# Weight-quarter sums on GpSimd instead of VectorE, and more value blocks through the Strassen path

## The chip, the core and the metric

The kernel runs on one core of one Trainium2 chip. The metric is device microseconds of one execution; the time of the kernel before is the median of three runs. Engines are named as the profile names them: PE (TensorE), DVE (VectorE), ACT (ScalarE), POOL (GpSimd) and SP (SyncE, which here only issues DMAs).

## The reference

Two transformer blocks over 512 tokens of width 1024, all in fp32. The first block is a hybrid attention mixer followed by a convolutional feed-forward stage:

```python
def conv_ffn(h, w_up, conv_w, conv_b, w_down):
    u = h @ w_up
    u = lax.conv_general_dilated(u, conv_w[:, None, :], window_strides=(1,), ...
    gate, val = jnp.split(u, 2, axis=-1)
    return (jax.nn.gelu(gate, approximate=True) * val) @ w_down
```

`w_up` is 1024 x 8192, so there are 4096 gate columns and 4096 value columns. The second block puts 16 meta tokens ahead (528 tokens) and runs two layers, each with two gated feed-forward stages of hidden width 2816 around a mixer:

```python
def swiglu(x, w_gate, w_up, w_down):
    return (jax.nn.silu(x @ w_gate) * (x @ w_up)) @ w_down
```

## The kernel before

**Number format.** Every weight and activation is split into a rounded high part H (a cast on ACT, L177) and a low part L = raw - H (a subtraction on DVE, L178). A product is three matmuls: H by H, H by low, low by H.

**Blocks.** The up-projections are done in blocks of 256 output columns, weights of 128 x 2048 that arrive as two raw tiles (`wraw`, 128 x 1024 each, three buffers). A block is done in one of two ways. The *direct* way (`direct`, gemm at L211) is 2 x 8 x 3 = 48 matmuls of 512 token columns (in the conv stage). The *Strassen* way (`strassen`) takes the 2 x 2 blocking of weights and tokens and needs seven products instead of eight: 7 x 4 x 3 = 84 matmuls of half the token columns (256 in the conv stage, 264 or 256 in the second block; L319 when a product opens an accumulator, L321 when it adds to one). The token side's sums are made once per stage (`strassen_y`). The weight side's four sums are made for each block, each of them one 128 x 512 addition or subtraction:

```python
S[:, :512] = A21 + A22             # L301
S[:, 512:] = S[:, :512] - A11      # L302
A12 = A12 - S[:, 512:]             # L305, in place
A11 = A11 - A21                    # L306, in place
```

S is the tile `ws` (one buffer). The split pieces go to tiles `wq` (four buffers; `w3` is a separate small pool for one quarter in the second block's stages). The order of products on PE is 0, 1, 4, 5, then product 3 of the *previous* block (its tail), then 2 and 6. Products 0 and 1 need the split of the raw r1 = (A11, A12); products 4 and 5 need the split of S; products 2 and 6 need the split of the r1 that L305 and L306 overwrote. On ACT, L330, L335 and L337 copy the accumulators of products 0, 4 and 5 out of PSUM; product 6 adds to the accumulator that L337 reads. On DVE, L333, L342 and L344 add accumulators to these copies.

**Which blocks.** In the conv stage, block b (0 to 15) has a gate part g and a value part v. Before, the gate parts of b = 2 to 14 and the value parts of odd b from 3 to 15 go the Strassen way: 13 + 7 = 20. In each of the four gated stages of the second block, gate and up parts of blocks 2 to 10 do: 4 x 9 x 2 = 72. Together 92.

**What sets the order.** A scheduler orders the instructions of each engine from the program's dependences, tile buffers and its own estimates; each engine then works its list strictly in that order. Between groups of blocks come slices of the down-projection (`down`, L211 on `hid`; accumulated by DVE at L1198 in the conv stage and L1325 in the second block). `conv` (L1134 on ACT, L1137 on DVE) and `hidden` (L1265, L1266) follow each block of the conv stage.

Of the kernel before, what the change touches and what calls it, by code (L numbers as in the profile page):

```python
# [132 lines left out]
class Builder:  # L133
# [157 lines left out]
    def strassen(self, src, Y, R, out, last, off=0, mid=None):  # L291


        nc, h = self.nc, R.n // 2
        r1 = self.wraw(src[:, :1024])
        r2 = self.wraw(src[:, 1024:], *self.rawpool)
        A11, A12, A21, A22 = r1[:, :512], r1[:, 512:], r2[:, :512], r2[:, 512:]
        W = [None] * 7
        W[0], W[1] = self.wtiles(r1, step=1024)
        S = (self.sumpool or self.qp).tile([P, 1024], F32, name="ws", tag="ws", bufs=1)  # L300
        nc.vector.tensor_add(out=S[:, :512], in0=A21, in1=A22)  # L301
        nc.vector.tensor_sub(out=S[:, 512:], in0=S[:, :512], in1=A11)  # L302
        W[4], W[5] = self.wtiles(S, step=1024)
        W[3], = self.wtiles(A22, **(dict(pool=self.qp, tag="w3", bufs=2, cols=512) if self.w3 else {}))
        nc.vector.tensor_sub(out=A12, in0=A12, in1=S[:, 512:])  # L305
        nc.vector.tensor_sub(out=A11, in0=A11, in1=A21)  # L306
        W[6], W[2] = self.wtiles(r1, back=True)

        def product(i, ps=None, tag="g"):

            new = ps is None
            ps = self.psum(tag)[:, :h] if new else ps
            for k in range(4):
                H, L = [t[:, k * P:(k + 1) * P] for t in W[i]]
                yH, yL = Y[i][k]
                for j, (a, b) in enumerate(((H, yH), (H, yL), (L, yH))):
                    first, last = k == 0 and j == 0, k == 3 and j == 2
                    if new:
                        nc.tensor.matmul(ps, lhsT=a, rhs=b, start=first, stop=last)  # L319
                    else:  # L320
                        nc.tensor.matmul(ps, lhsT=a, rhs=b, start=False, stop=last, skip_group_check=True)  # L321
            return ps

        u = self.qp.tile([P, 2, TT // 2], F32, name="cu", tag="cu", bufs=2)
        v = self.qp.tile([P, TT // 2], F32, name="cv", tag="cv", bufs=2)
        u1, u2, v = u[:, 0, :h], u[:, 1, :h], v[:, :h]
        a0, b0 = R.off + off, R.off + off + h
        A, B = slice(a0, b0), slice(b0, b0 + h)
        X = product(0)
        nc.scalar.copy(out=u1, in_=X)  # L330
        out = out()
        Z = product(1, tag="o")
        nc.vector.tensor_add(out=out[:, 0, A], in0=u1, in1=Z)  # L333
        Y5 = product(4)
        nc.scalar.copy(out=v, in_=Y5)  # L335
        product(5, X)
        nc.scalar.copy(out=u2, in_=X)  # L337
        self.end()
        if mid:
            mid()  # L340
        product(2, Y5)
        nc.vector.tensor_add(out=out[:, 0, B], in0=u2, in1=Y5)  # L342
        product(6, X)
        nc.vector.tensor_add(out=out[:, 1, B], in0=v, in1=X)  # L344

        def tail():
            product(3, X)
            last(out[:, 1, A], X)

        self.tail = tail  # L350
        return A, out
# [772 lines left out]
    def conv_ffn(self):  # L1124
        nc, A, R, qp = self.nc, self.A, R1, self.qp
        ys, rb = self.prenorm_end()
        hid, self.hb, self.w3, self.gub = {}, 4, False, 3
        off = 2 - NMETA

        def conv(u, j):  # L1130

            a = qp.tile([P, 2, SEQ], F32, name="ca", tag="ca", bufs=2)
            for n in range(2):
                nc.scalar.activation(out=a[:, n], in_=u[:, n, 2:SEQ + 2], func=AF.Identity, scale=self.v("conv_w2", j + n),  # L1134
                                     bias=self.v("conv_b", j + n))
                for i in (1, 0):
                    nc.vector.scalar_tensor_tensor(out=a[:, n], in0=u[:, n, i:i + SEQ], scalar=self.v(f"conv_w{i}", j + n),  # L1137
                                                   in1=a[:, n], op0=ALU.mult, op1=ALU.add)
            return a

        def direct(u, w, n, Rp):
            for t, o, m in self.gemm(w, n, ys, Rp):
                nc.scalar.copy(out=u[:, n, o + off:o + off + m], in_=t[:, :m])

        def product(b, fast, mid=None):
            if fast:
                a, u = self.strassen(A["w_up"][b], self.Y, R, buf, lambda o, p: nc.scalar.copy(out=o, in_=p), off, mid)
            else:
                if mid:
                    mid()  # L1150
                u = buf()
                w = self.qblock(A["w_up"][b])
                for n in range(2):
                    direct(u, w, n, R)
                    self.end()
            return u

        def post(b, g, v):
            a = conv(g, 2 * b)
            nc.scalar.activation(out=a, in_=a, func=AF.Gelu_apprx_tanh)  # L1160
            c = conv(v, 32 + 2 * b)
            nc.vector.tensor_mul(out=c, in0=c, in1=a)
            hid[2 * b], hid[2 * b + 1] = self.hidden(c, NMETA)

        def buf():
            u = self.gu()
            nc.vector.memset(u[:, :, 0:2], 0.0)
            return u

        def up(b):  # L1170
            if b == 0:
                g, v, hid["g"] = buf(), buf(), buf()
                W = [*self.pre, self.qblock(A["w_up"][1], pool=qp, tag="h", bufs=self.hb, cols=2 * TT, step=1024)]
                self.prenorm_y(self.rlast)
                for Rp in R.parts:
                    for u, w in zip((g, v, hid["g"]), W):
                        for n in range(2):
                            direct(u, w, n, Rp)
            elif b == 1:
                g = hid.pop("g")  # L1180
                v = product(17, False, self.flush)
            else:
                if b == 2:
                    self.Y = self.strassen_y(ys, R, True)
                g = product(b, b < 15)
                v = product(16 + b, b % 2, self.flush)
            self.pending = lambda: post(b, g, v)

        def down(ci, k0, nk, nb):
            W = self.wblock(A[f"w_down{ci}"][nb], nk, step=1024)  # L1190
            for n in range(2):
                t = 2 * nb + n
                ps = self.gemm(W, n, [hid[k0 + k] for k in range(nk)], R, tag="sg"[n])[0][0]
                self.end()
                if k0 == 0:
                    nc.scalar.copy(out=self.x[:, t, NMETA:], in_=ps)
                else:
                    nc.vector.tensor_add(out=self.x[:, t, NMETA:], in0=self.x[:, t, NMETA:], in1=ps)  # L1198

        def last(ci, k0, nk):  # L1200
            W = self.last_w(A[f"w_down{ci}"], nk, ("t3", "t4"))
            hs = [hid[k0 + k] for k in range(nk)]
            self.prenorm("ffn1_norm_0", False)
            acc = self.tmp("acc2", 1)

            def products(R, between=()):
                self.gemm_pairs(W, hs, R, lambda ps, t: self.post_tile(ps, acc, t, R, True), between)

            def post(R):
                self.postnorm(acc, "ffn_post_norm", R, R2.parts[R1.parts.index(R)], self.xd, None)  # L1210

            self.halves(R1.parts, products, post, self.ffn_w("ffn1_0"), R2.parts)

        self.ffn_order(CHUNKS1, up, down, last)

    def last_w(self, src, nk=4, spare=("t3",)):
# [660 lines left out]
```

## Time and profile before

| what | value |
|---|---|
| median of 3 runs | 3096.11 us (3094.0 to 3098.47) |
| profiled execution | 3098.56 us |
| its span, first to last instruction | 3096.8 us |
| mean granted PE clock | 0.996 of full speed |
| PE busy | 3060.1 us, 99% |
| DVE busy | 2191.9 us, 71% |
| ACT busy | 1511.0 us, 49% |
| POOL busy | 30.9 us, 1% |

The table is to be read with care: a share of busy time is an average over all stages, and PE's matmuls overlap, so that the mean length of one matmul is longer than the spacing between two.

### The profile page before, as it was taken

The page shows a single profiled execution, that of the slowest core. Times are in us where ns is not written, and L with a number is a line of the kernel's source. Part 1 is how long each engine was busy: PE and PEld are TensorE (multiplying, and loading weights), DVE is VectorE, ACT ScalarE, POOL GpSimd, SP SyncE. Part 2 cuts the span into 40 slices and gives each one's busy share as a digit, 9 for nine tenths or more (in the row PEclk, how much of TensorE's full clock was granted, in tenths as well). Part 3 has the DMA queues.
Part 4 walks back from the last instruction along what each step waited for, and adds up shares of the span by engine and source line. Part 5 has one row for each costly group of instructions (what it writes and reads, how often), then busy time and mean ns, then how long its engine had stood idle before and what let it go on. Part 6 is the DMA issues. An engine that isn't in the chain of part 4 may idle for free.

```text
span 3096.8 us, 54004 instructions
## 1 busy us (share of the span) xinstructions
PE 3060.1 (99%) x21936; PEld 2825.3 (91%) x21936; DVE 2191.9 (71%) x4109; ACT 1511.0 (49%) x2916; POOL 30.9 (1%) x64
## 2 busy tenths in 40 slices
PE   8999999999999999999999999999999999999998
PEld 6777789989898999999899999999999988899998
DVE  6244648888887887766766877767777585687775
ACT  5435546655555544445543544444444464354443
POOL 1100000000000000000000000000000000000000
PEclk9999999999999999999999999999999999999999
DMA  6222245223224223232121223232323211223232
GB/s 228 71 84 96 101 158 178 82 99 107 95 96 143 76 97 109 89 103 97 45 70 65 96 93 103 93 117 76 102 96 115 92 58 56 79 83 103 96 110 75
DMA packets 97081, 304.34 MB, mean 98 GB/s; under 512 B 12327, under 2 KB 20927, under 8 KB 96704
## 3 DMA queue, kind: packets, MB, share of 16 engines
q1 hardware_dynamic: 90512, 286.63, 27.7%
q0 software_dynamic: 2720, 7.78, 0.8%
q10 hardware_dynamic: 3600, 6.49, 0.7%
q8 instruction: 171, 2.80, 0.4%
q14 instruction: 78, 0.64, 0.1%
HBM read 290.34 MB, written 14.45 MB: 98 GB/s over the span
## 4 chain that ended last, share of the span: by engine, by line
PE 93%; DMA 2%; DVE 2%; ACT 2%; issue 1%; ACTq 0%; DVEq 0%; SPq 0%
PE ps_g L211 38%; PE ps_g L321 17%; PE ps_g L319 8%; PE ps_s L211 8%; PE ps_g L249 7%; PE ps_o L319 4%; PE ps_o L249 1%; DMA tmp_p<-gates 1%; PE ps_s L1641 1%; PE ps_s L1698 1%; PE ps_o L1677 1%; PE ps_g L656 1%; DMA num<-in_x 1%; PE ps_o L1707 1%; DMA wraw<-in_ffn_w_gate 0%
## 5 line engine op out<-in xcount | busy, mean ns | idle before, releaser
L178 DVE TENSOR_TENSOR wqL<-wraw,wqH 128x512 fp32r<-128x512 f32 (+1 forms) x668 | 603.8, 917 | 319.3 <-ACT wqH L177 311.8
L177 ACT CAST wqH<-wraw 128x512 fp32r<-128x512 f32 (+1 forms) x668 | 525.9, 803 | 544.1 <-PE ps_g L211 337.2
L211 PE MATMUL ps_g<-yH,wqH 128*128 128x264 f32 (+2 forms) x1664 | 489.5, 329 | 0.0
L211 PE MATMUL ps_g<-yH,wqL 128*128 128x264 f32 (+2 forms) x1664 | 484.9, 327 | 0.3 <-DVE wqL L178 0.2
L211 PE MATMUL ps_g<-yL,wqH 128*128 128x264 f32 (+2 forms) x1664 | 484.6, 325 | 0.4 <-DVE yL L457 0.4
L211 PEld LDWEIGHTS ps_g<-yH,wqH 128*128 128x128 f32 x1664 | 290.0, 189 | 29.8 <-issue 4.8
L211 PEld LDWEIGHTS ps_g<-yL,wqH 128*128 128x128 f32 x1664 | 291.7, 189 | 26.8 <-DVE yL L457 1.1
L211 PEld LDWEIGHTS ps_g<-yH,wqL 128*128 128x128 f32 x1664 | 290.0, 189 | 27.1 <-DVE wqL L178 0.7
L321 PE MATMUL ps_g<-t,wqH 128*128 128x264 f32 (+1 forms) x1632 | 303.1, 283 | 0.0
L321 PEld LDWEIGHTS ps_g<-t,wqH 128*128 128x128 f32 x1632 | 252.7, 188 | 1.8
L321 PE MATMUL ps_g<-t,wqL 128*128 128x264 f32 (+1 forms) x816 | 230.5, 282 | 0.0
L177 ACT CAST wqH<-ws 128x1024 fp32r<-128x1024 f32 x92 | 96.8, 1052 | 118.5 <-issue 36.6
L321 PEld LDWEIGHTS ps_g<-t,wqL 128*128 128x128 f32 x816 | 153.9, 189 | 0.0
L211 PE MATMUL ps_s<-hL,wqH 128*128 128x264 f32 (+1 forms) x544 | 141.3, 317 | 0.0
L211 PE MATMUL ps_g<-hL,wqH 128*128 128x264 f32 (+1 forms) x544 | 141.2, 317 | 0.0
L211 PE MATMUL ps_g<-hH,wqL 128*128 128x264 f32 (+1 forms) x544 | 141.1, 317 | 0.0
L211 PE MATMUL ps_s<-hH,wqL 128*128 128x264 f32 (+1 forms) x544 | 141.1, 317 | 0.0
L211 PE MATMUL ps_g<-hH,wqH 128*128 128x264 f32 (+1 forms) x544 | 141.0, 316 | 0.0
L211 PE MATMUL ps_s<-hH,wqH 128*128 128x264 f32 (+1 forms) x544 | 140.9, 316 | 0.0
L319 PE MATMUL ps_g<-t,wqH 128*128 128x264 f32 (+1 forms) x736 | 136.7, 283 | 0.0
L178 DVE TENSOR_TENSOR wqL<-ws,wqH 128x1024 fp32r<-128x1024 f32 x92 | 112.4, 1222 | 9.2 <-ACT wqH L177 6.2
L1325 DVE SCALAR_TENSOR_TENSOR xres<-ps_g,xres 128x264 f32<-128x264 f32 (+2 forms) x168 | 71.3, 451 | 65.4 <-PE ps_g L211 35.3
(434 smaller groups left out, 7815.0 us busy)
## 6 DMA issues: line engine op xcount, KB each, us to landing
wraw<-in_ffn_w_gate SPq DMA_DIRECT2D x88, 512.0 KB, 3.5
wraw<-in_ffn_w_up SPq DMA_DIRECT2D x88, 512.0 KB, 3.5
wraw<-in_ffn_w_down SPq DMA_DIRECT2D x88, 512.0 KB, 3.5
wraw<-in_w_in SPq DMA_DIRECT2D x86, 512.0 KB, 3.5
wraw<-in_w_up SPq DMA_DIRECT2D x64, 512.0 KB, 3.6
wraw<-in_w_down SPq DMA_DIRECT2D x32, 512.0 KB, 3.5
wraw<-in_w_gate SPq DMA_DIRECT2D x24, 512.0 KB, 3.7
tmp_p<-gates ACTq DMA_DIRECT2D x24, 256.0 KB, 3.5
```

The lines of the kernel that those rows point to most:

```text
L177: self.nc.scalar.copy(out=H, in_=raw)
L178: self.nc.vector.tensor_sub(out=L, in0=raw, in1=H.bitcast(F32))
L211: self.nc.tensor.matmul(t[:, :m], lhsT=a, rhs=b[:, o:o + m], start=(k == 0 and i == 0), stop=(k == nk - 1 and i == 2))
L249: self.nc.tensor.matmul(q[:, :m], lhsT=a, rhs=b[:, o:o + m], start=(k == 0 and i == 0), stop=(k == nk - 1 and i == 2))
L319: nc.tensor.matmul(ps, lhsT=a, rhs=b, start=first, stop=last)
L321: nc.tensor.matmul(ps, lhsT=a, rhs=b, start=False, stop=last, skip_group_check=True)
L656: nc.tensor.matmul(ps[:, :256], lhsT=a[:, ts], rhs=w, start=(k == 0 and i == 0), stop=(k == KD - 1 and i == 2))
L1325: nc.vector.scalar_tensor_tensor(out=self.x[:, t, o:o + m], in0=pt[:, :m], scalar=0.5, in1=self.x[:, t, o:o + m], op0=ALU.mult, op1=ALU.add)
L1641: nc.tensor.matmul(ps[:nq, :e - a], lhsT=qm[r], rhs=k[2][r, a:e], start=False, stop=not dg)
L1677: nc.tensor.matmul(ops[:nq, :P], lhsT=aT[:, j * P:j * P + nq], rhs=V[:, j], start=(j == 0), stop=False)
L1698: nc.tensor.matmul(ps[:cnt, :e - a], lhsT=k[:, j * P:j * P + cnt], rhs=q[:, a:e], start=True, stop=True)
L1707: nc.tensor.matmul(ops[r0:n, :P], lhsT=w[:cnt, off[j] + i0 + r0:off[j] + i0 + n], rhs=V[:cnt, j], start=(j == 0), stop=(j == i))
```

## The change

The four sums of `strassen` are issued on GpSimd instead of VectorE, for every Strassen block; and the condition for value blocks becomes that of gate blocks.

```diff
         S = (self.sumpool or self.qp).tile([P, 1024], F32, name="ws", tag="ws", bufs=1)
-        nc.vector.tensor_add(out=S[:, :512], in0=A21, in1=A22)
-        nc.vector.tensor_sub(out=S[:, 512:], in0=S[:, :512], in1=A11)
+        nc.gpsimd.tensor_add(out=S[:, :512], in0=A21, in1=A22)
+        nc.gpsimd.tensor_sub(out=S[:, 512:], in0=S[:, :512], in1=A11)
         W[4], W[5] = self.wtiles(S, step=1024)
         W[3], = self.wtiles(A22, **(dict(pool=self.qp, tag="w3", bufs=2, cols=512) if self.w3 else {}))
-        nc.vector.tensor_sub(out=A12, in0=A12, in1=S[:, 512:])
-        nc.vector.tensor_sub(out=A11, in0=A11, in1=A21)
+        nc.gpsimd.tensor_sub(out=A12, in0=A12, in1=S[:, 512:])
+        nc.gpsimd.tensor_sub(out=A11, in0=A11, in1=A21)
         W[6], W[2] = self.wtiles(r1, back=True)
...
                 g = product(b, b < 15)
-                v = product(16 + b, b % 2, self.flush)
+                v = product(16 + b, b < 15, self.flush)
```

The scheduler makes a new order from this. The first place is DVE's list around block b = 5 of the conv stage, from the release of block 4's outputs to the evacuations of the gate part (`wraw` raw weights, `ws` the sums, `wqL` low parts, `gu` block outputs, `xres` the residual stream). Before:

```order
L1167 MEMSET gu 128x2x2
L301 TENSOR_TENSOR ws<-wraw 128x512
L1198 TENSOR_TENSOR xres<-xres,ps_g 128x512
L178 TENSOR_TENSOR wqL<-wraw,wqH 128x512 x2
L302 TENSOR_TENSOR ws<-ws,wraw 128x512
L333 TENSOR_TENSOR gu<-cu,ps_o 128x256
L178 TENSOR_TENSOR wqL<-wraw,wqH 128x1024
L305 TENSOR_TENSOR wraw<-wraw,ws 128x512
L306 TENSOR_TENSOR wraw<-wraw 128x512
L178 TENSOR_TENSOR wqL<-ws,wqH 128x1024
L342 TENSOR_TENSOR gu<-cu,ps_g 128x256
```

After:

```order
L1198 TENSOR_TENSOR xres<-xres,ps_g 128x512
L178 TENSOR_TENSOR wqL<-wraw,wqH 128x512 x2
L333 TENSOR_TENSOR gu<-cu,ps_o 128x256
L178 TENSOR_TENSOR wqL<-wraw,wqH 128x1024
L178 TENSOR_TENSOR wqL<-ws,wqH 128x1024
L342 TENSOR_TENSOR gu<-cu,ps_g 128x256
```

The sums of the value part are gone from DVE's list, and the rest keeps its order. They stand on POOL's list as L301, L302, L305, L306, once for each of 98 blocks, with nothing of another kind behind the first of them.

The second place is ACT's list around block b = 4, whose value part was direct and is now a Strassen block. Before:

```order
L330 COPY cu<-ps_g 128x256
L177 CAST wqH<-wraw 128x512 x2
L335 COPY cv<-ps_g 128x256
L177 CAST wqH<-wraw 128x512
L337 COPY cu<-ps_g 128x256
L177 CAST wqH<-wraw 128x512
```

After:

```order
L330 COPY cu<-ps_g 128x256
L177 CAST wqH<-wraw 128x1024
L335 COPY cv<-ps_g 128x256
L177 CAST wqH<-ws 128x1024
L337 COPY cu<-ps_g 128x256
L1134 ACTIVATE ca<-gu,vecs 128x512
L177 CAST wqH<-wraw 128x512
L330 COPY cu<-ps_g 128x256
L177 CAST wqH<-wraw 128x512 x2
L335 COPY cv<-ps_g 128x256
```

The cast of the value part's sums (`wqH<-ws`) now stands between L335 and L337 of the gate part, as it already did at odd b.

## Rows read from the trace of the kernel before

**Rows 1.** The page's parts 1 and 2: engines, and 40 slices of the span.

```profile
PE 3060.1 (99%) x21936; PEld 2825.3 (91%) x21936; DVE 2191.9 (71%) x4109; ACT 1511.0 (49%) x2916; POOL 30.9 (1%) x64
...
PE   8999999999999999999999999999999999999998
...
PEclk9999999999999999999999999999999999999999
```

**Rows 2.** The waits of PE: line, waited for, us in total, times, longest.

```profile
PE ps_g L211 <- ACT oH L366: 8.9, 2, 8.5
...
PE ps_g L321 <- DVE gu L344: 0.6, 1, 0.6
```

**Rows 3.** The chain that ended last, 560 to 600 us: start us, us, what (b = 2).

```profile
571.24 1.42 PE ps_g L319 x12
572.66 1.43 PE ps_o L319 x12
574.09 1.42 PE ps_g L319 x12
575.50 4.26 PE ps_g L321 x36
579.76 5.55 PE ps_g L211 x24
585.32 1.43 PE ps_g L321 x12
586.74 5.55 PE ps_g L211 x24
```

**Rows 4.** Groups of DVE: names, count | busy us, mean ns | idle before, releaser.

```profile
L178 DVE TENSOR_TENSOR wqL<-ws,wqH 128x1024 fp32r<-128x1024 f32 x92 | 112.4, 1222 | 9.2 <-ACT wqH L177 6.2
...
L301 DVE TENSOR_TENSOR ws<-wraw 128x512 f32<-128x512 f32 x92 | 63.6, 691 | 67.5 <-DMA wraw<-in_ffn_w_gate 30.1 <-DMA wraw<-in_ffn_w_up 21.5 <-DMA wraw<-in_w_up 15.7
```

**Rows 5.** Groups of POOL, the same columns.

```profile
masks.py:199 POOL TENSOR_SCALAR_AFFINE_SELECT ident<-ident 128x128 f32<-128x128 f32 x1 | 0.3, 317 | 0.1
...
L1866 POOL MEMSET const-bfloat16-1.0<- 128x1 bf16 x1 | 0.1, 101 | 0.0
```

**Rows 6.** Timeline of DVE, 666.5 to 674 us (b = 5, value part's sums).

```profile
666.90 0.69 DVE L301 TENSOR_TENSOR ws<-wraw 128x512 f32<-128x512 f32 x1 [2.05 <-DMA wraw<-in_w_up]
667.51 0.68 DVE L1198 TENSOR_TENSOR xres<-xres,ps_g 128x512 f32<-128x512 f32 x1
...
670.67 1.23 DVE L178 TENSOR_TENSOR wqL<-wraw,wqH 128x1024 fp32r<-128x1024 f32 x1 [0.34 <-ACT wqH L177]
```

**Rows 7.** Timeline of ACT, 671.5 to 679 us (the same block).

```profile
672.42 1.05 ACT L177 CAST wqH<-ws 128x1024 fp32r<-128x1024 f32 x1 [0.92 <-PE ps_g L321]
673.38 0.36 ACT L337 COPY cu<-ps_g 128x256 f32<-128x256 f32 x1
...
678.29 1.14 ACT L177 CAST wqH<-wraw 128x512 fp32r<-128x512 f32 x2 [0.99 <-PE ps_o L319]
```

**Rows 8.** The chain, 664 to 690 us: products 5, 2 and 6 of that gate part.

```profile
671.09 4.38 PE ps_g L321 x36
```

**Rows 9.** Timeline of SP's DMA issues, 565 to 575 and 660 to 668 us.

```profile
571.30 0.33 SPq L191 DMA_DIRECT2D wraw<-in_w_up  x1
...
663.13 0.33 SPq L191 DMA_DIRECT2D wraw<-in_w_up  x1
```

**Rows 10.** Busy time by stretch: window, us, then each engine's busy us (count), PEclk.

```profile
666.80:698.00 31.20, 31.20 (x219) 28.99 (x218) 26.17 (x40) 16.34 (x26) 0.00 (x0) 1.00 0.30 102
1798.00:1830.20 32.20, 32.20 (x267) 32.20 (x266) 24.03 (x37) 14.30 (x23) 0.00 (x0) 1.00 0.30 99
2787.00:2818.00 31.00, 31.00 (x218) 28.89 (x217) 24.19 (x35) 14.37 (x24) 0.00 (x0) 1.00 0.24 85
1300.00:1326.00 26.00, 26.00 (x216) 26.00 (x215) 19.22 (x30) 12.59 (x22) 0.00 (x0) 1.00 0.31 102
2998.00:3024.00 26.00, 26.00 (x199) 24.94 (x198) 21.18 (x31) 13.20 (x23) 0.00 (x0) 1.00 0.31 103
```

**Rows 11.** Timeline of DVE, 1108 to 1114 us (first blocks of a gated stage).

```profile
1108.64 0.69 DVE L301 TENSOR_TENSOR ws<-wraw 128x512 f32<-128x512 f32 x1 [3.09 <-DMA wraw<-in_ffn_w_gate]
...
1113.26 0.42 DVE L344 TENSOR_TENSOR gu<-cv,ps_g 128x264 f32<-128x264 f32 x1
```

## The prediction

> **What bounds the kernel now.** I read the page's first two parts, then PE's waits, then the chain that ended last, then stretches and timelines. PE is busy 99% of the span, in nearly every slice, at full clock [rows 1]. Its waits are few: the longest is 8.9 us at the very start, and in the Strassen stages only one of 0.6 us, on DVE's L344, stands out [rows 2]. So PE's own work sets the time. DVE has 29% to spare and POOL nearly everything [rows 1], so lifting work from DVE pays nothing by itself; only fewer PE microseconds pay, and a preparation that comes late costs. The chain shows what PE pays: pieces of matmuls that follow each other without a gap [rows 3].
>
> **PE's part.** The condition is read with care. Value blocks that were Strassen before: odd b from 3 to 15, seven. After: every b from 2 to 14, thirteen. The seven even ones are new, but b = 15 falls out. Net six more: 98 Strassen blocks where there were 92. A Strassen block costs 1.42 + 1.43 + 1.42 for products 0, 1 and 4, 4.26 for 5, 2 and 6, and 1.43 for the tail: 9.96 us. A direct block costs 5.55 + 5.55 = 11.10 us [rows 3]. The difference is 1.14 us, and 6 x 1.14 = 6.84 us leave PE. This is on the path wherever PE doesn't wait.
>
> **DVE's part.** It loses 4 x 92 sums of 0.69 us [rows 4], some 254 us. PE isn't waiting for them, so I cost this at nothing, with one exception: L301 on DVE waits for its raw tile (3.09 us idle at 1105.55 to 1108.64) and holds everything behind it, down to L344, which ends at 1113.68 [rows 11] and is the wait of 0.6 us above. On POOL it holds nothing of DVE's. Gain 0.6 us, at least 0. The direct blocks' weight splits turn into Strassen splits; both are hidden behind PE as the odd blocks' are now.
>
> **POOL's part.** 4 x 98 = 392 sums of 128 x 512. The trace has no such operation on POOL. Below, DVE's 0.69 us is a bound. The nearest POOL row is one affine select of 128 x 128 at 0.317 us, against 0.101 us for a single element [rows 5]: 1.70 ns for an element, so 0.10 + 512 x 1.70 ns = 0.97 us with one input, and 0.10 + 2 x 0.87 = 1.84 us if a second input is read after the first. I take 4 x 0.317 = 1.27 us, between the two, and keep 0.69 and 1.84. The Trainium skill, GPSIMD Engine Reference, section "Elementwise — side-by-side cycle accounting", has 4497 ns for an addition of 2048 fp32 elements on GpSimd; a quarter, 1.12 us, would be an estimate from it. By that the sum below stays the same, since it is hidden in either case.
>
> Nothing else is queued on POOL in these stages, so its sums delay only each other and those who wait for them. I checked the tightest such place, the value part behind its gate part. The raw tile arrives at 666.90 and the first sum starts at once [rows 6]; ACT casts the sums at 672.42, when product 5 has given back its buffer, and then L337 takes 0.36 us from 673.38 [rows 7]. Product 6 adds to the accumulator that L337 reads; products 5, 2 and 6 start at 671.09 and take 4.38 us, so product 6 starts at about 674.01 [rows 8]. The cast must therefore start by 674.01 - 0.36 - 0.96 = 672.69. Two sums on POOL end at 666.90 + 2 x 1.27 = 669.44, over 3 us ahead. L305 and L306 follow the split that starts at 670.67 and takes 1.23 us [rows 6]: 671.90 + 2.54 = 674.44, and their cast waits for PE until 678.29 [rows 7]. Both delays are covered. If this cover is gone, ACT's L337 is late first, and PE stops at product 6.
>
> The even blocks' value parts now stand like the odd ones', in PE's order and in ACT's. The one new place without an older twin is b = 2. Its second raw tile is issued at 571.30 [rows 9]; the like issue at 663.13 [rows 9] arrived at 666.90 [rows 6], 3.8 us later. So: 575.1 + 2.54 = 577.6, cast and L337 until 577.6 + 0.96 + 0.36 = 578.9, while product 6 of the gate part is due at 575.50 + 2/3 x 4.26 = 578.3 [rows 3]. Cost 0.6 us; bounds 0 (the tile is issued earlier) and 2 (DVE, busy there without a gap, is late as well).
>
> **The sum.** -6.84 - 0.6 + 0.6 = -6.8 us. The profiled execution, 3098.56 us (span 3096.8 and 1.8 around it), would become 3091.7. The median of the runs is 2.45 us under it: 3096.11 - 6.8 = **3089.3 us**.
>
> **The rivals.**
>
> *The cover is thin in the value blocks.* With the upper bound and one long DVE instruction (1.22 us [rows 4]) ahead of each sum, two sums take 2 x (1.84 + 1.22) = 6.1 us and end at 673.0, past 672.69. PE then loses 0.3 us in each of 13 value blocks, 4 us; with two DVE instructions in the way 1 us, 13 us more. Time 3091 to 3102, about 3094. For it: raw tiles arrive only 5.5 us before the cast. Against: it needs the upper bound each time.
>
> *The two engines take turns.* Most of DVE's work there has two inputs in SBUF, as the sums have. If neither can run while the other does, their times add up. The stretch of the conv stage with two Strassen blocks lasts 31.2 us with DVE busy 26.17 [rows 10]; less 8 x 0.69 that is 20.7, and 8 POOL sums fit until one takes (31.2 - 20.7) / 8 = 1.31 us. From there on DVE and POOL together are the bound and the kernel gets **slower**. In the last stretch of the gated stages (26.0 us, DVE 21.18) the point is (26.0 - 15.7) / 8 = 1.29. At 1.58 us, midway from 1.31 to 1.84, a conv stretch takes 20.7 + 12.6 = 33.3, 2.1 more, 13 times: 27 us. The gated stretches of 31.0, of 26.0 early and of 26.0 late [rows 10] grow by 0.3, 0.3 and 2.3, some 7, 6 and 2 times: 8.5 us. Those of 32.2 still fit. Together +35 - 6.8 = +29: 3125 us. At 1.84 it would be above 3190, which I hold for remote: DVE instructions that read PSUM need not take turns, and DVE's busy time counts overlaps of neighbours twice (0.69 us long, the next one 0.61 later [rows 6]). Against it too: 1.27 lies just under both points. For it: just under is no comfort, and no row shows POOL and DVE at work together. The Trainium skill, SBUF — State Buffer, section "Who interferes with whom", states such a rule, that a VectorE instruction with two SBUF inputs and a GpSimd instruction that reads SBUF block each other for a whole instruction. No run here shows it yet; by it this rival's mechanism holds, and its point of decision stands as above.
>
> *The change does less than it says.* This one isn't open: six blocks, not seven, and the sum has it.
>
> **How the numbers follow.** Forecast (all hidden): chance 0.60, own range 3086 to 3093 (the b = 2 stall from 0 to 2, L344's 0.6 from 0 to 1, and 2 us of scatter in three runs). Thin cover: 0.22. Taking turns: 0.18. The range should leave out no more than 2 in 10: from 3086 over the forecast and the thin cover (to 3102) into the beginning of the third, 3106. A measurement of this kernel can tell about 0.2%, 6.2 us, from no change. The forecast's middle is 6.8, so it lies at this edge: I give it 0.42 for faster and 0.18 for the same. The thin cover is the same, 0.22; together 0.40. Taking turns is slower, 0.18.
>
> **What would show it.** Right: PE's busy time down by about 7 us; two-block stretches of the conv stage all near 31 us; 392 POOL sums of 0.97 to 1.5 us, DVE's idle time up; no new entry above 2 us among PE's waits. Thin cover: PE waits on ACT's L337 some 13 times, and POOL's L302 ends after product 5. Taking turns: DVE's L178 of `ws` longer than 1.22 us, or POOL's sums far over 1.3 us, conv stretches of 33 us and PE waiting for `wqL`. Wrong altogether: a gain over 10 us, which no term here could give, or a loss with PE as busy as before.

## The result and the profile after

The changed kernel takes **3170.6 us** (median of 4 runs, 3164.3 to 3171.8) beside 3097.1 of the kernel before in the same comparison: ratio 1.0232, 95% interval 1.0220 to 1.0244, about 72 us slower (73 by the medians). The forecast was 3089.3, 7 us faster, with a range that ended at 3106.

Part 1 of the page after, the first line of its part 4 (the chain that ended last, by engine), and the same line of the page before:

```profile
PE 3077.8 (97%) x22152; PEld 2840.5 (90%) x22152; DVE 2193.9 (69%) x3765; ACT 1505.9 (48%) x2934; POOL 674.5 (21%) x456
...
PE 50%; issue 12%; DMA 12%; DVE 11%; POOL 10%; ACT 5%; POOLq 0%; ACTq 0%; DVEq 0%; SPq 0%
```

```profile
PE 93%; DMA 2%; DVE 2%; ACT 2%; issue 1%; ACTq 0%; DVEq 0%; SPq 0%
```

PE's count grew by 216 matmuls, as six more Strassen blocks make it, but its busy time didn't fall, and its share of the chain went from 93% to 50%. DVE has lost 368 sums, 254 us of work [rows 4], and is as busy as before: 2193.9 us against 2191.9 [rows 1]. So its other instructions must have become longer. The groups of POOL and of DVE (count | busy us, mean ns | idle before, releaser) show it:

```profile
L306 POOL TENSOR_TENSOR wraw<-wraw 128x512 f32<-128x512 f32 x98 | 206.3, 2105 | 0.0
L302 POOL TENSOR_TENSOR ws<-ws,wraw 128x512 f32<-128x512 f32 x98 | 157.8, 1610 | 7.7
L305 POOL TENSOR_TENSOR wraw<-wraw,ws 128x512 f32<-128x512 f32 x98 | 145.1, 1480 | 313.3 <-issue 247.0 <-DVE wqL L178 62.4
L301 POOL TENSOR_TENSOR ws<-wraw 128x512 f32<-128x512 f32 x98 | 138.4, 1412 | 1789.2 <-DMA wraw<-in_ffn_w_gate 838.9 <-PE ps_g L211 379.0 <-DMA wraw<-in_w_up 354.2
```

```profile
L178 DVE TENSOR_TENSOR wqL<-ws,wqH 128x1024 fp32r<-128x1024 f32 x98 | 163.0, 1663 | 88.0 <-ACT wqH L177 87.9
...
L178 DVE TENSOR_TENSOR w3L<-wraw,w3H 128x512 fp32r<-128x512 f32 x72 | 96.0, 1333 | 161.0 <-ACT w3H L177 159.3 <-PE ps_g L321 1.6
L1315 DVE TENSOR_TENSOR gu<-gu 128x1056 f32<-128x1056 f32 x27 | 60.2, 2228 | 3.7 <-ACT gu L1309 3.7
```

Four operations of one size have means from 1.41 to 2.11 us; the split of `ws` went from 1.22 us [rows 4] to 1.66. The waits of PE (line, waited for, us, times, longest) name who is late:

```profile
PE ps_g L321 <- ACT cu L337: 37.3, 50, 1.7
...
PE ps_g L321 <- ACT cu L330: 6.8, 8, 2.5
```

**Turn-taking, seen in one place.** Timelines of POOL and of DVE (start us, us) in a gated stage:

```profile
1214.79 1.29 POOL L305 TENSOR_TENSOR wraw<-wraw,ws 128x512 f32<-128x512 f32 x1 [7.34 <-issue]
1216.03 2.27 POOL L306 TENSOR_TENSOR wraw<-wraw 128x512 f32<-128x512 f32 x1
```

```profile
1214.57 0.42 DVE L333 TENSOR_TENSOR gu<-cu,ps_o 128x264 f32<-128x264 f32 x1
1214.91 2.25 DVE L178 TENSOR_TENSOR wqL<-ws,wqH 128x1024 fp32r<-128x1024 f32 x1
1217.08 2.60 DVE L178 TENSOR_TENSOR wqL<-wraw,wqH 128x512 fp32r<-128x512 f32 x2
```

L305 comes first and takes its 1.29 us, to 1216.08. DVE's split of `ws`, recorded from 1214.91, lasts until 1217.16: 1.08 us after L305's end, about its own 1.22. L306, recorded from 1216.03, ends at 1218.30, 1.14 us after the split, about its own 1.28. The two splits that follow take 2.60 us instead of 1.28 and end after L306. Each engine's record contains the other's turn. L333, L342 and L344, which have one input in PSUM, keep their length: of the 294 in the changed kernel 89 ran wholly beside sums, with a mean of 0.413 us, and none at all is longer than 0.431.

**The loop that got too long.** The chain of the same stage (start us, us, what):

```profile
1189.30 4.58 DMA wraw<-in_ffn_w_gate
...
1194.04 1.28 POOL ws L301
...
1195.40 1.65 POOL ws L302
...
1197.11 1.30 POOL wraw L305
1198.41 2.24 POOL wraw L306
...
1200.67 3.61 DMA wraw<-in_ffn_w_up
...
1204.36 0.63 ACT w3H L177
...
1206.20 1.25 DVE gu L1315
...
1214.79 1.29 POOL wraw L305
1216.07 2.24 POOL wraw L306
...
1218.33 0.63 ACT wqH L177
```

There is no PE in it. The chain's 1.25 us of L1315 are a part of that instruction, which lasts 2.35 us there. There are three raw tiles; the fourth sum frees the tile into which the next block's second load goes. From the first sum to the end of the fourth it is 1194.04 to 1200.65, 6.6 us. Then the load takes 3.6 us, and the next block's casts wait for it. (Between L1315 and L305 the chain has 7.3 us of "issue", in which the profile names no releaser. What ends just before L305 is DVE's split of the first raw tile, which L305 overwrites: it lasts from 1213.44 to 1214.66.) The same places with the sums on VectorE, in the timeline of the version with more value blocks alone (below):

```profile
1197.62 0.69 DVE L301 TENSOR_TENSOR ws<-wraw 128x512 f32<-128x512 f32 x1 [1.24 <-DMA wraw<-in_ffn_w_gate]
...
1201.63 0.69 DVE L306 TENSOR_TENSOR wraw<-wraw 128x512 f32<-128x512 f32 x1
...
1208.11 1.25 DVE L1315 TENSOR_TENSOR gu<-gu 128x1056 f32<-128x1056 f32 x1
```

Here it is 1197.62 to 1202.32, 4.7 us, and L1315 takes 1.25 us, where its mean in the changed kernel is 2.23. ACT's wait for these loads, from its waits in the changed kernel,

```profile
ACT w3H L177 <- DMA wraw<-in_ffn_w_up: 174.6, 34, 7.2
```

is half as long in that version:

```profile
ACT w3H L177 <- DMA wraw<-in_ffn_w_up: 87.2, 25, 5.7
```

In the conv stage the chain runs through DVE as well:

```profile
663.53 1.63 POOL ws L302
665.18 1.05 ACT wqH L177
666.26 1.16 DVE wqL L178
...
667.53 1.78 DVE ca L1137
...
675.29 2.14 DVE wqL L178 x2
...
677.66 1.05 ACT wqH L177
678.71 0.28 ACT cu L337
679.03 1.68 PE ps_g L321 x12
```

The cast of `ws` at 677.66 had waited 1.3 us for POOL's L302; L337 stands behind it on ACT and PE's product 6 behind L337: the order of events that the prediction had worked out, [rows 6 to 8], but with the cover gone.

### The profile page after: what moved, and what is told of

It reads as the page before. It is cut to its first block, busy times and chain, and to the rows that moved or that the text cites. A ratio compares the mean times of both kernels' runs of the same rounds, so it can differ in the third digit from the quotient of the medians.

```text
span 3170.0 us, 54937 instructions
## 1 busy us (share of the span) xinstructions
PE 3077.8 (97%) x22152; PEld 2840.5 (90%) x22152; DVE 2193.9 (69%) x3765; ACT 1505.9 (48%) x2934; POOL 674.5 (21%) x456
## 4 chain that ended last, share of the span: by engine, by line
PE 50%; issue 12%; DMA 12%; DVE 11%; POOL 10%; ACT 5%; POOLq 0%; ACTq 0%; DVEq 0%; SPq 0%
PE ps_g L211 25%; PE ps_g L249 7%; DMA wraw<-in_ffn_w_gate 5%; DMA wraw<-in_ffn_w_up 4%; PE ps_g L321 4%; POOL wraw L306 4%; ACT wqH L177 3%; DVE wqL L178 3%; POOL wraw L305 2%; POOL ws L302 2%; POOL ws L301 2%; PE ps_g L319 2%; PE ps_s L211 2%; DMA wraw<-in_w_up 1%; DVE gu L1315 1%
## 5 line engine op out<-in xcount | busy, mean ns | idle before, releaser
L178 DVE TENSOR_TENSOR wqL<-wraw,wqH 128x512 fp32r<-128x512 f32 (+1 forms) x668 | 664.8, 1008 | 303.6 <-ACT wqH L177 293.9
L301 POOL TENSOR_TENSOR ws<-wraw 128x512 f32<-128x512 f32 x98 | 138.4, 1412 | 1789.2 <-DMA wraw<-in_ffn_w_gate 838.9
L321 PE MATMUL ps_g<-t,wqH 128*128 128x256 f32 (+1 forms) x1776 | 336.8, 287 | 44.1 <-ACT cu L337 37.3
L211 PEld LDWEIGHTS ps_g<-yH,wqH 128*128 128x128 f32 x1568 | 271.7, 189 | 26.3 <-issue 4.7
L321 PE MATMUL ps_g<-t,wqL 128*128 128x256 f32 (+1 forms) x888 | 252.2, 284 | 0.0
L178 DVE TENSOR_TENSOR wqL<-ws,wqH 128x1024 fp32r<-128x1024 f32 x98 | 163.0, 1663 | 88.0 <-ACT wqH L177 87.9
L305 POOL TENSOR_TENSOR wraw<-wraw,ws 128x512 f32<-128x512 f32 x98 | 145.1, 1480 | 313.3 <-issue 247.0
L178 DVE TENSOR_TENSOR w3L<-wraw,w3H 128x512 fp32r<-128x512 f32 x72 | 96.0, 1333 | 161.0 <-ACT w3H L177 159.3
L306 POOL TENSOR_TENSOR wraw<-wraw 128x512 f32<-128x512 f32 x98 | 206.3, 2105 | 0.0
L302 POOL TENSOR_TENSOR ws<-ws,wraw 128x512 f32<-128x512 f32 x98 | 157.8, 1610 | 7.7
L319 PE MATMUL ps_g<-t,wqH 128*128 128x264 f32 (+1 forms) x784 | 145.6, 283 | 0.0
```

Of the source, the lines that this page charges most:

```text
L178: self.nc.vector.tensor_sub(out=L, in0=raw, in1=H.bitcast(F32))
L211: self.nc.tensor.matmul(t[:, :m], lhsT=a, rhs=b[:, o:o + m], start=(k == 0 and i == 0), stop=(k == nk - 1 and i == 2))
L301: nc.gpsimd.tensor_add(out=S[:, :512], in0=A21, in1=A22)
L302: nc.gpsimd.tensor_sub(out=S[:, 512:], in0=S[:, :512], in1=A11)
L305: nc.gpsimd.tensor_sub(out=A12, in0=A12, in1=S[:, 512:])
L306: nc.gpsimd.tensor_sub(out=A11, in0=A11, in1=A21)
```

## The experiments

Unless it is said otherwise, a kernel here is the version of experiment 1 (more value blocks, the sums on VectorE) with one edit. "Held up" is the theory that the engines block each other, "late sums" that the sums are only longer and their waiters late.

**1. More value blocks alone.**

```diff
-                v = product(16 + b, b % 2, self.flush)
+                v = product(16 + b, b < 15, self.flush)
```

> Only the value blocks change; the four sums stay on VectorE. Both theories, the one that GpSimd and VectorE hold each other up when both work on SBUF ('held up') and the one that the sums are merely late for who waits for them ('late sums'), put the whole loss on GpSimd and keep the -6.8 us of six more Strassen blocks: 3090 us beside 3097. The third theory, that seven more blocks in a row leave the weights' preparation without cover, expects 3100 us or more.

3090.5 us beside 3098.4: ratio 0.9976 (0.9967 to 0.9984), 7.4 us faster (5.0 to 10.2). The prediction's 6.84 is confirmed, and the third theory falls. GpSimd's sums thus cost 1.0232 / 0.9976 = 1.0257, some 79 us. DVE's durations for what follows: `wqL<-ws` 1220 ns, `w3L` 684, L1315 1252.

**2. The sums alone** (value blocks as before).

```diff
-        nc.vector.tensor_add(out=S[:, :512], in0=A21, in1=A22)
+        nc.gpsimd.tensor_add(out=S[:, :512], in0=A21, in1=A22)
...
```

> Only the sums move to GpSimd; the value blocks stay as in the kernel before. If the two parts add up, the loss over the version with more value blocks alone (80 us for 98 Strassen blocks) comes for 92 blocks: 3097 + 75 = 3172 us, so that the more blocks are worth about as little here as the two kernels differ: 3168 to 3177 us. If seven more blocks in a row were what has no cover on GpSimd, 3150 us or less.

3156.1 us, ratio 1.0195 (1.0179 to 1.0210): between the two expectations. Against the changed kernel (1.0232) the six blocks that gave 7 us with sums on VectorE cost 11 us with sums on GpSimd. The parts don't add up; that both eat the same slack is the likely reason, and not shown.

**3. One pair of sums at a time.** First the two of `ws` (L301, L302) on GpSimd; then instead the two that overwrite the first raw tile (L305, L306):

```diff
-        nc.vector.tensor_sub(out=A12, in0=A12, in1=S[:, 512:])
-        nc.vector.tensor_sub(out=A11, in0=A11, in1=A21)
+        nc.gpsimd.tensor_sub(out=A12, in0=A12, in1=S[:, 512:])
+        nc.gpsimd.tensor_sub(out=A11, in0=A11, in1=A21)
```

> More value blocks, and only the two sums that make ws on GpSimd; the two that overwrite the first raw tile stay on VectorE. 'Late sums': the ws pair has the most slack (products 0 and 1 run before ws is needed), the other pair feeds the last weights cast and frees the second raw tile, so little is lost here: 3092 to 3105 us. 'Held up': two of four sums work beside VectorE's splits of the first raw tile, so close to half of the loss: 3120 to 3140 us.

> More value blocks, and only the two sums that overwrite the first raw tile on GpSimd; the two of ws stay on VectorE. 'Late sums': nearly the whole loss, 3140 to 3165 us. 'Held up': half of it or somewhat more, since the trace shows the fourth sum at 2.27 us beside the split of ws: 3125 to 3145 us.

3115.5 us (ratio 1.0061, 1.0048 to 1.0075) and 3133.1 us (1.0115, 1.0101 to 1.0129): 25 and 43 us over the first experiment, neither of them small. Together 68, the two pairs at once 79. The `ws` pair comes out 4 us under the range of "held up" and 10 over that of "late sums"; the other pair within the first and under the second.

**4. GpSimd work that nobody waits for.** The sums stay on VectorE. When `ws` is there, GpSimd copies one column of it into a tile of its own and then works on that tile alone: 14 additions of 128x128 as in the diff, or 50 fills (`memset`), or 14 multiplications by 0 (`tensor_scalar`) in a block.

```diff
+        d = self.qp.tile([P, P], F32, name="idle", tag="idle", bufs=1)
+        nc.gpsimd.tensor_copy(out=d[:, :1], in_=S[:, 1023:])
+        nc.gpsimd.memset(d, 0.0)
+        for _ in range(14):
+            nc.gpsimd.tensor_add(out=d, in0=d, in1=d)
         W[4], W[5] = self.wtiles(S, step=1024)
```

> More value blocks and all sums on VectorE, and beside them in every Strassen block some 5 to 6 us of GpSimd additions on a tile of its own, started when ws is there, for which nobody waits. 'Held up': VectorE's instructions with two SBUF inputs get longer (the split of ws 1.22 to about 1.7 us in the mean, as in the changed kernel) and the kernel loses 15 us or more against the one with more value blocks alone: 3105 to 3170 us. 'Late sums': nobody waits for this work, so no change against that kernel: 3088 to 3094 us, and VectorE's durations stay.

> As the version with added additions on GpSimd for which nobody waits, but GpSimd only fills its own tile (128x128 memsets that read nothing, 50 in a block, 5 us or more). 'Held up' by a path that both engines share for reads and writes: VectorE's two-input instructions get longer again and 10 us or more are lost against 3090. If only GpSimd's reads hold VectorE up, durations stay and the time is 3088 to 3094 us. 'Late sums' expects the latter too.

> As the version with added additions for which nobody waits, but GpSimd's operation has one SBUF input (a tile times 0, 14 of 128x128 in a block). If any GpSimd read of SBUF holds VectorE up, about 3105 to 3120 us as with the additions; if it takes two inputs, as with the fills, 3088 to 3094 us and VectorE's durations as before.

Additions: 3120.4 us (1.0076, 1.0061 to 1.0091), 30 over the first experiment. Multiplications: 3100.3 (1.0010, 1.0001 to 1.0020), 10 over it, below what was expected of them and above nothing. Fills: 3089.4 (0.9977, 0.9968 to 0.9986), nothing. Groups of POOL and DVE with the additions:

```profile
L307 POOL TENSOR_TENSOR idle<-idle 128x128 f32<-128x128 f32 x1372 | 984.0, 717 | 107.8
```

```profile
L178 DVE TENSOR_TENSOR wqL<-ws,wqH 128x1024 fp32r<-128x1024 f32 x98 | 127.5, 1301 | 0.6 <-ACT wqH L177 0.5
...
L311 DVE TENSOR_TENSOR wraw<-wraw 128x512 f32<-128x512 f32 x98 | 80.1, 817 | 0.0
```

and with the fills:

```profile
L306 POOL MEMSET idle<- 128x128 f32 x4900 | 1004.1, 205 | 282.1
```

```profile
L178 DVE TENSOR_TENSOR wqL<-ws,wqH 128x1024 fp32r<-128x1024 f32 x98 | 119.7, 1221 | 4.5 <-ACT wqH L177 0.8
...
L310 DVE TENSOR_TENSOR wraw<-wraw 128x512 f32<-128x512 f32 x98 | 67.1, 685 | 0.0
```

A thousand microseconds of fills leave DVE's durations as they were; as many of additions lengthen them. So it is GpSimd's operations that read SBUF that hold VectorE up, and that alone costs time though nobody waits for the result. (The next block's L301 waited for the copied column of `ws`, 7.4 us in all beside the additions; it waited 23.8 us beside the fills, where that cost nothing.) These instructions are short; DVE gets its turn sooner than beside a sum of 1.28 us, so the 30 us are no measure of what the changed kernel loses this way.

**5. Lateness without contention.** The sums stay on VectorE; GpSimd copies one column after each pair and rewrites one column of the result with itself, and what reads the result waits for that. A second version puts six fills of its own tile in between.

```diff
+        nc.gpsimd.tensor_copy(out=d[:, :1], in_=S[:, 1023:])
+        nc.gpsimd.tensor_copy(out=S[:, :1], in_=S[:, :1])
         W[4], W[5] = self.wtiles(S, step=1024)
...
+        nc.gpsimd.tensor_copy(out=d[:, :1], in_=r1[:, 511:512])
+        nc.gpsimd.tensor_copy(out=r1[:, 512:513], in_=r1[:, 512:513])
+        nc.gpsimd.tensor_copy(out=r1[:, :1], in_=r1[:, :1])
+        nc.gpsimd.tensor_copy(out=d[:, :1], in_=r2[:, :1])
         W[6], W[2] = self.wtiles(r1, back=True)
```

> More value blocks, sums on VectorE, but what reads them is let go late: after each pair of sums GpSimd copies one column and rewrites one column of the result, and only then do ScalarE's casts start (and the second raw tile come free). That delays each pair by about 1 us, as two GpSimd sums beside nothing would (2.6 instead of 1.4 us), with almost no GpSimd work on SBUF. 'Late sums': 1 us twice in each of 98 blocks is most of what the changed kernel adds, so a good part of the 80 us comes back: 3110 us or more. 'Held up': next to nothing, 3089 to 3096 us.

> The same with six fills of a tile of its own ahead of each release, 1.2 us more: each pair now comes some 2.2 us late, more than the changed kernel's own sums are late with all contention (3.0 and 3.6 instead of 1.4 us, so 1.6 and 2.2). 'Late sums': the whole loss or more, 3150 us or above. 'Held up': under a quarter of it, 3090 to 3110 us. In between, both share, and the difference to 3090 is the part of being late.

3117.7 us (1.0067, 1.0052 to 1.0082) and 3167.9 us (1.0231, 1.0214 to 1.0248), with DVE's durations unchanged (`wqL<-ws` 1222 and 1222 ns). Lateness with DVE not held up costs 27 us in the first, and 77 in the second. But the second didn't delay what its text says. Timeline of POOL, and one line of DVE's:

```profile
1199.44 1.05 POOL L304 COPY idle<-ws 128x1 f32<-128x1 f32 x1 [11.58 <-DVE ws L302]
1200.43 0.66 POOL L307 COPY ws<-ws 128x1 f32<-128x1 f32 x1
1201.03 1.52 POOL L306 MEMSET idle<- 128x128 f32 x6
1202.50 0.18 POOL L315 COPY wraw<-wraw 128x1 f32<-128x1 f32 x1
...
1204.05 1.51 POOL L314 MEMSET idle<- 128x128 f32 x6
1205.62 0.18 POOL L317 COPY idle<-wraw 128x1 f32<-128x1 f32 x1
```

```profile
1199.23 1.22 DVE L178 TENSOR_TENSOR wqL<-wraw,wqH 128x1024 fp32r<-128x1024 f32 x1
```

The copies themselves stood behind DVE: L304's 1.05 us end 0.04 us after this split. Of the 588 one-column copies of this run, 274 started while a DVE instruction with two SBUF inputs ran, and nearly all of these ended 0.04 us after it; the others take 0.18 us in the median. The fills came behind the release of `ws` (L307), not ahead of it. What they delayed by 1.5 us is L317, the last reader of the second raw tile, and in the block shown the release of the other pair (L315) as well. It is so in the whole run: the fills follow L307 in all 98 blocks, and L317 ends 3.2 us after the last sum in the median, where it is 1.6 in the first version. So 50 us hang on these, and the next runs take the waiters apart.

**6. Which waiter.** (a) Only the second raw tile is held: after L306 GpSimd fills its own tile eight times, then reads one column of the raw tile. (b) Only ACT's casts of both pairs are late; a column of zeros, made by the fills and then added, now fixes the order. (c) Only the cast of `ws` is late. The diffs of (a) and of (c); (b) has the like of (c) for both pairs:

```diff
+        nc.gpsimd.tensor_copy(out=d[:, :1], in_=r1[:, 511:512])
+        for _ in range(8):
+            nc.gpsimd.memset(d, 0.0)
+        nc.gpsimd.tensor_add(out=d[:, :1], in0=d[:, :1], in1=r2[:, :1])
         W[6], W[2] = self.wtiles(r1, back=True)
```

```diff
+        nc.gpsimd.tensor_copy(out=d[:, :1], in_=S[:, 1023:])
+        for _ in range(6):
+            nc.gpsimd.memset(d, 0.0)
+        nc.gpsimd.tensor_add(out=S[:, :1], in0=S[:, :1], in1=d[:, :1])
         W[4], W[5] = self.wtiles(S, step=1024)
```

> More value blocks, sums on VectorE, and only the second raw tile held some 2.5 us longer in each block (GpSimd fills a tile of its own eight times after the last sum and then reads one column of the raw tile). 'Raw loop' (the loss comes from the next block's load, which waits for this tile): 40 us or more, 3130 us and up. 'Late casts' (it comes from casts that wait for the sums): 3089 to 3100 us, the loads have that slack.

> More value blocks, sums on VectorE, the second raw tile free as soon as they are done, but ScalarE's casts of both pairs let go some 2.5 to 3 us late (GpSimd: one column copied, six fills, a zero added to one column). 'Raw loop': 3090 to 3110 us. 'Late casts': 3140 us and up.

> The same for the cast of ws alone, the other pair as it is. 'Late casts': about half of the version with both pairs late, 3110 to 3140 us, or more if the delay of ws also delays the casts behind it on ScalarE. 'Raw loop': 3089 to 3100 us.

(a) 3136.7 us (1.0128, 1.0111 to 1.0145), 46 over the first experiment; (b) 3120.6 (1.0077, 1.0062 to 1.0092), 30; (c) 3123.5 (1.0088, 1.0073 to 1.0103), 33. The raw tile was held 2.7 us in the median of the blocks, and the cast of `ws` let go 2.6 us after its last sum. Both waiters cost: the raw tile more, of the casts that of `ws` alone, since making the other pair's late as well adds nothing that these runs can tell. Neither theory had it whole.

**7. The changed kernel with its last two sums swapped**, so that the raw tile comes free after the third.

```diff
-        nc.gpsimd.tensor_sub(out=A12, in0=A12, in1=S[:, 512:])
         nc.gpsimd.tensor_sub(out=A11, in0=A11, in1=A21)
+        nc.gpsimd.tensor_sub(out=A12, in0=A12, in1=S[:, 512:])
```

> The changed kernel with its last two sums in the other order, so that the second raw tile comes free one sum sooner (1.3 to 2.1 us) and product 2's weights one sum later. 'Raw loop': 15 us or more under the changed kernel's 3170.6, 3155 us or less. 'Late casts': the same or more, 3170 to 3190 us.

3157.9 us, ratio 1.0197 (1.0181 to 1.0212) against the changed kernel's 1.0232: 11 us back by the ratios, 13 by the medians. The load's wait for this tile is part of the loss; nearer to what the raw loop expected than to the other, if a little short of it.

**Where each version loses.** ACT's timeline has one L335 COPY of `cv` for each of the 98 Strassen blocks, so the distance from one start to the next is what a block takes. This table is worked out from those starts: distances less those of the first experiment, summed. "Gated, middle" is from the 4th to the 13th of the 18 blocks in each of the four gated stages, where down products stand between pairs of blocks; "gated, ends" the first three and the last five distances of each, the last of them without down products; "elsewhere" up to the first block and between stages. These are single executions, up to 7 us off their medians.

```
us over the first experiment   conv   gated, middle   gated, ends   elsewhere   sum
changed kernel                 16.7       28.7           23.7         11.2      80.3
pair of ws on GpSimd           17.3        0.6            2.7         11.0      31.4
other pair on GpSimd           15.6        5.4            8.3          7.0      36.3
added additions                21.7        0.0            2.7          4.1      28.5
late, with fills (exp. 5)      28.2        1.1           40.4          7.3      77.0
raw tile held                   9.3        0.1           33.3          3.9      46.6
cast of ws late                16.7        0.0           17.0          3.4      37.0
changed, last sums swapped     18.0        6.6           28.9         11.3      64.8
```

In the conv stage, where DVE is busiest [rows 10], anything costs: contention alone, a late `ws` alone, a held raw tile alone; and they don't add up. In the middle of the gated stages none of these three costs anything. GpSimd's own sums do, contention and lateness at once, and there mostly with both pairs; freeing the raw tile one sum sooner takes that 28.7 down to 6.6, with 5 more at the ends. At the ends the held tile alone makes a loss of this size, and the late cast alone 17.0. The version of experiment 5 that loses as much in sum as the changed kernel loses it elsewhere, at the ends: the equal totals don't make it the same loss. The loss "elsewhere" was not taken apart.

**The order of the lists.** With the sums on GpSimd the scheduler also made another order for the conv stage. On ACT the cast of `ws` for the value part stands ahead of the gate part's L337 in all 13 pairs of the changed kernel and of experiments 3 and 7, as it did before at odd b; in experiment 1 and the versions with added additions or fills it does so in 4 pairs, and L337 comes first in the other 9. So in the conv stage the table's first three rows and its last compare two orders as well, and no run separates the order from the sums. In the four gated stages, where most of the loss lies, ACT's list is the same in both, but for 2 of 193 entries in the first and 12 of 192 in the last.

**The granted clock.** A further rival is that PE's waits bring its clock down and that the clock makes the loss. In the changed kernel the granted clock falls to the lower of its two levels (1.2 GHz) three times in these stages, 10.3 us in all, close behind waits of 2.48, 1.89 and 1.74 us; in experiment 1 it doesn't fall there. The first stretch (us, then busy us and count of PE, PEld, DVE, ACT, POOL, then PEclk):

```profile
578.80:582.40 3.60, 3.60 (x17) 3.60 (x18) 3.60 (x5) 2.13 (x4) 0.63 (x1) 0.53 0.40 85
```

PE does 17 matmuls in it, and 33 in the same stretch of experiment 1 at the full clock. So the 10.3 us at half speed cost about 5 of the 80 us (an estimate from these counts), and the clock is a small part. The versions with longer single waits lose more this way: 30.7 us at the lower level in the late version with fills, 17.1 with the cast of `ws` late, 13.7 with the raw tile held.

**8. Versions that beat both kernels.** Sums on VectorE, and block 15's value part by Strassen too; then its gate part as well.

```diff
-                g = product(b, b < 15)
-                v = product(16 + b, b % 2, self.flush)
+                g = product(b, True)
+                v = product(16 + b, True, self.flush)
```

> Sums on VectorE as before, and the value block 15 by Strassen as well: net seven more blocks than in the kernel before. Each of six was worth 7.9 / 6 = 1.3 us in the version with more value blocks alone, so about 3089 us, 1 us under that version, if the last block has the same cover; block 15 comes just before the last products, and if its preparation has none there, 3090 to 3093 us.

> As the version with all value blocks, and the gate block 15 too: net eight more blocks than before. About 3088 us if it is covered as the others, 3090 to 3095 us if the last gate block's preparation stands in the way of the loads for the last products.

3088.3 us (0.9967, 0.9955 to 0.9980) and 3087.1 (0.9966, 0.9953 to 0.9978). Both beat the two kernels of this case: the second is 10.5 us faster than before (6.8 to 14.6). Among themselves and the first experiment the intervals don't separate them; the expected steps of about 1 us are smaller than these runs can tell apart.

## Why the prediction failed, step by step

- **PE's part** was right: six blocks, 6.84 us, measured alone 7.4 (5.0 to 10.2).
- **DVE's part**, relief worth nothing, wasn't put to the test: the relief itself didn't take place. Beside experiment 1, DVE lost sums of 270 us, and its other instructions are 236 us longer in sum, as they stood behind GpSimd's. The wait of 0.6 us on L344 did go.
- **POOL's part, the duration.** 1.27 us was right for a sum beside nothing: the shortest of L301, L302, L305 and L306 are 1.264, 1.283, 1.267 and 1.282 us. That it is so close is luck, since it came from a row of another operation with one input. As what a sum takes at work it was wrong: the means are 1.41 to 2.11.
- **POOL's part, "Both delays are covered": the step that failed.** It took the raw tile's arrival at 666.90 from the trace of before and moved only what comes after it. But that arrival hangs on the sums and splits of the block before, through three raw tiles. With later sums the tile comes later, each block passes its delay on (the loop above shows it in a gated stage), and the 3 us of cover are used up from both sides. In the stretch of the conv chain above (a line of POOL's timeline, one of ACT's):

```profile
674.48 1.46 POOL L301 TENSOR_TENSOR ws<-wraw 128x512 f32<-128x512 f32 x1 [5.71 <-DMA wraw<-in_w_up]
```

```profile
675.99 0.37 ACT L335 COPY cv<-ps_g 128x256 f32<-128x256 f32 x1 [0.21 <-PE ps_g L319]
```

The first sum starts 1.5 us ahead of L335, which follows product 4. Before, the first sum was 4.2 us ahead of product 5 [rows 6, 8]. The sums aren't alone in this: the lead of the first sum over L335 is 4.4 us in the median of 6 value parts before, 2.3 of 13 in experiment 1 and 1.4 of 13 in the changed kernel. More value blocks took the larger part of it, which the prediction also had at nothing; PE lost nothing by that in experiment 1, where L337 mostly stands ahead of the late cast. That a raw tile held longer costs 46 us by itself was shown by (a) of experiment 6. "Its sums delay only each other and those who wait for them" was the second fault: they also delayed DVE instructions that wait for nothing of theirs, which experiment 4 showed.
- **b = 2** was priced at 0.6 us, on L337 and product 6. PE has no wait there; its wait in this block is one of 2.5 us on L330, ahead of product 5, which the prediction didn't have. One block, so of little weight.
- **The rival of thin cover** had the right path, L337 and product 6, and its signs came: in the conv stage PE waits there 12 times (it said 13), 9.0 us in all, and the cast waits for L302 and not for product 5. For that stage it was near (4 to 13 us; measured 16.7), but by its reckoning two sums had to take 6.1 us. They took 3.3 in the median of the value parts; what had shrunk was the lead. PE waits there another 38 times behind the conv stage. Of the gated stages, 52 of 80 us, the rival said nothing.
- **The rival that the engines take turns** had the right mechanism and side, with a chance of 0.18. Two of its signs came: `wqL<-ws` at 1.66 us, sums far over 1.3. Two didn't: conv stretches of 33 us, and PE waiting for `wqL` (0.2 us in all). The Trainium skill, SBUF — State Buffer, section "Who interferes with whom", states it: a VectorE instruction with two SBUF inputs contends with a GpSimd instruction that reads SBUF, and not with one that only writes. The traces agree in both halves: 1.22 to 1.66 us beside the sums, 1.22 beside the fills. But the price was that of throughput, and by it the gated stretches of 32.2 us "still fit" and conv stretches go to 33. Measured: a conv pair with its down products went from 31.0 us to about 31.8 and a gated one from 32.1 to 33.7, with DVE idle a third of the time there. Pairs without down products went from 26.3 (25.5 in the last stage) to some 28 to 30, nearer to the 2.3 us more that it had for late ones. By throughput a sum of 1.65 us, the mean of all four, gives some 3140 (an estimate by the prediction's own sum); measured 3170.6. What the gated middle shows is a price of latency: a turn of some 1.1 us in the loop load, sums, release, load. That is read from the timelines and from experiment 7, and no run measures it by itself. One argument against this rival was a wrong reading, too: a stretch's busy time counts overlaps once (26.17 us in [rows 10], where the durations add up to 28.4), so that taking 8 x 0.69 off it takes off too much. Without the sums DVE is busy 21.6 us there, and the point of decision is 1.20 us and not 1.31: below the 1.27 of the forecast.
- **"Wrong altogether: ... a loss with PE as busy as before"**: this sign came as well. PE is busy 3077.8 us beside 3060.1 before and 3055.6 in experiment 1, with the same 22152 matmuls as the latter. So 22 of the 80 us lie in matmul records that are longer or overlap less, and 58 in gaps.

What stays open is how much each of contention and lateness has of the 79 us, what the new order adds in the conv stage, and how much of it all comes through the clock. The edits that isolate one are not of the changed kernel's size: the additions are shorter than its sums, and the raw tile was held 2.7 us (from L306's end at 1293.99 to 1296.66) where in the changed kernel the way from the first sum to the fourth is 1.9 us longer. They don't add up either. A fourth raw tile, which might open the loop with the sums left on GpSimd, was not tried.

## What to carry to other kernels

Relieving an engine that is 70% busy while PE sets the time promises nothing, and it can cost when the work moves to an engine that has to take turns with it at SBUF, as here: count the turn of the other's instruction on each, both ways, and price it as latency and not as a share of time. Before a delay is called covered, follow what the late instruction frees, not only who reads its result: with few buffers, the next load's start moves too, and a cover read from the old trace goes with it. Where two parts of a change are offered, run each alone; here one gave 7 us and the other took 79.

## What the runs showed of the hardware beyond that

- GpSimd's fills of 128x128 (0.205 us each, 1004 us in all) left DVE's durations as they were; additions of the same size did (0.397 us at the shortest, 0.717 in the mean, so they too stood behind DVE).
- GpSimd's multiplications, with one SBUF input, held VectorE up less than its additions, with two: `wqL<-ws` 1.260 us beside the multiplications, 1.301 beside the additions, at about the same 990 us of work. Whether it is the number of inputs is not shown: one multiplication is also longer (0.527 us at the shortest, 0.397 an addition).
- A copy of a single column on GpSimd took 1.05 us where a split of VectorE was running, and 0.18 us where none was (L304 and L315 in the timeline of experiment 5): even one column waits out the whole instruction. A hand-over through GpSimd isn't free, however small the work.
